# Row products of a scan step handed out one filler unit later, in a hybrid Mamba-2 / pooling trunk on one core

## The chip, the core and the metric

The kernel runs on one core of a Trainium2 chip. Five engines work side by side, each through its own queue in order: TensorE (PE in the profile, with its weight loads as PEld), VectorE (DVE), ScalarE (ACT), GpSimd (POOL) and SyncE (SP), which here issues most DMA transfers. The metric is the device time of one execution in microseconds (us); shown is the median of several runs. Beside these, one execution was profiled.

## The reference

The program is one step of a two-layer decoder trunk over 1024 prompt tokens and 64 sample tokens (8 sequences of 8), width 1024, all in float32. Layer 0 is a Mamba-2 (SSD) mixer, layer 1 a multi-scale causal pooling mixer; each is modulated by a conditioning vector, normalised, gated and added to the residual, and a final RMSNorm closes. What matters here is the chunked scan of layer 0, with 8 groups of 4 heads (head size 64, state size 128) and chunks of 128 tokens:

```python
acum = jnp.cumsum(dt * A, axis=2)
decay = jnp.where(mask, jnp.exp(seg), 0.0)          # seg = acum_t - acum_s
CB = jnp.einsum('bctgn,bcsgn->bctsg', C, B)
y_intra = jnp.einsum('bctsgr,bcsgrp->bctgrp', CB[..., None] * decay, xdt)
chunk_states = jnp.einsum('bctgn,bctgr,bctgrp->bcgrpn', B, decay_end, xdt)
def step(h, inp):
    s, d = inp
    return d[..., None, None] * h + s, h
y_inter = jnp.einsum('bctgn,bctgr,bcgrpn->bctgrp', C, jnp.exp(acum), h_prev)
y = y_intra + y_inter
```

Then come the skip term, a gate with silu(z), a group RMSNorm over 256 channels, and the output projection. The sample sequences run the same scan from a stored state.

## The kernel before

Activations lie with channels on the partitions and 1088 tokens (1024 + 64) along the free axis. Large products take float32 as a high and a low part, so one product is three matmuls (`mm1`, L190 to L192). The front of the kernel projects most columns; then the SSD stage (`ssd_layer`, L1547) runs the scan of the 8 groups, one after the other, while it deals out **filler units** between the scan's steps: pieces of big products that do not depend on the present scan. `beside` (L1589) yields them: first the input projections of the groups in BESIDE (one unit is one token chunk, 8 x 3 matmuls of 368 or 352 columns), the last tile of these in eight smaller units, and then the output projections by parts (one unit is 4 x 3 matmuls).

`scan_group` (L525) is a generator; each `yield` ends a **hand-out**, after which `ssd_layer` takes as many filler units as `FILL[g]` (L53) says at that place. Its pieces:
- `front(c)`, for a chunk of 128 tokens (c = 8 is the sample): the product of C and B (L573), transposes of x and B (L576) on PE; on ACT the decays as a Relu and an Exp (L581, L582), exp(acum) (L565) and a copy of the transposed B (Bt, L593); on DVE the masked C·B (L584), M (L587), the scaled x (xd, L589) and C times exp(acum) (ea, L602). M, xd and ea have three buffers, Bt two, the PSUM tile `tr` two. It also issues the load of acum two chunks ahead (L549, L552).
- `states(c)`, for the chunks c and c + 1: two products of Bt and xd into one PSUM tile S (L615), the decay of h on POOL (hd, L623), and the sum on DVE (L624, or a copy at L620 for a group's first).
- `rows(c)`, the **row products** of the same two chunks: M times xd (L637) and, into the same PSUM tile, h times ea (L641), with each half of 64 output rows in one half of the array; then DVE adds the skip term (L607). The first chunk uses the h from before `states(c)`, the second the first h made there.
- `sample_inter` (L645), `back_sample` (L663) and `state_sample` (L687) do the sample's part: the stored states times C (Z, L656), the sample's row products (L670) and its new states (L692, added at L695).
- After that the gate (L732), squares and their sum (zsum, L769), the mean square by PE (L741), the inverse root, and the scaled rows (L753), stored to DRAM (L756). The last two hand-outs of a group are taken as `rest` within the next group, after its first filler unit (L1564) and at its fourth hand-out (L1567).

The order of the instructions in each engine's queue is planned when the program is built, from the order of the program, the dependences and an estimate of when operands are ready; `issue_after` adds an edge to it by hand. So the order on an engine may differ from that of the program. The tiles of activations are slots of one list, taken from its head and returned to its end (`Slots`, L66). At one place (L1568) the loads of the next group's B, C and x into slots are issued, for the groups whose tiles were made early (5 and 7).

Of the kernel before, what the change touches and what calls it, by code (L numbers as in the profile page):

```python
# [49 lines left out]
         ("z", 7))  # L50
BESIDE = (1, 2, 3, 4, 6)

FILL = (((1,) * 10 + (2,),) * 4 + ((1,) * 9 + (4, 5),) + ((3, 2, 2, 2, 2, 2, 2, 2, 2, 2, 3),) * 2 + ((2, 2, 2, 1, 1, 1, 1, 1, 2, 2, 1),))  # L53
WIDE = 1223


# [43 lines left out]
class Build:  # L100
# [424 lines left out]
    def scan_group(self, g, T):  # L525
        nc, tk, gp, pp = self.nc, self.tk, self.gs, self.pp
        B, C, xs, zs = T[0], T[1], T[2:4], []
        hsl, h0 = [], []

        def load_z():  # L530
            for q in range(2):
                zs.append(self.slots.get("z"))
                nc.sync.dma_start(zs[q], self.zsd[2 * g + q])

        def load_h0():
            for i in range(2):
                t = self.slots.get("h0")
                nc.sync.dma_start(t[:, :1024], self.io["h0T"][g][:, 1024 * i:1024 * i + 1024])
                hsl.append(t)
                h0.append(t[:, :1024].rearrange("p (b r q) -> p b r q", b=4, r=4))  # L540
# [64 lines left out]
        def evac_y(py, q, tok, L):  # L605
            y = xs[q]
            nc.vector.scalar_tensor_tensor(out=y[:, tok], in0=y[:, tok], scalar=self.vec[:, V_D + 2 * g + q:V_D + 2 * g + q + 1], in1=py[:, :L],  # L607
                                           op0=ALU.mult, op1=ALU.add)

        def states(c, F):  # L610

            S = pp.tile([P, 512], F32, tag="S", bufs=1, name=self.name("S"))
            for i in range(2):
                xde, Bt = F[i][3:5]
                nc.tensor.matmul(S[:, 256 * i:256 * i + 256], Bt, xde.rearrange("p r q -> p (r q)"), start=True, stop=True)  # L615
            for i in range(2):
                cd, Si = F[i][5], S[:, 256 * i:256 * i + 256]
                hn = gp.tile([P, 4, 64], F32, tag="h", bufs=3, name=self.name("h"))
                if h[-1] is None:
                    ins = nc.vector.tensor_copy(hn.rearrange("p r q -> p (r q)"), Si)  # L620
                else:
                    hd = gp.tile([P, 4, 64], F32, tag="hd", bufs=1, name=self.name("hd"))
                    nc.gpsimd.tensor_tensor(out=hd, in0=h[-1], in1=cd.unsqueeze(2).to_broadcast([P, 4, 64]), op=ALU.mult)  # L623
                    ins = nc.vector.tensor_tensor(out=hn, in0=hd, in1=Si.rearrange("p (r q) -> p r q", r=4), op=ALU.add)  # L624
                h.append(hn)
            self.hins = ins.ins

        def rows(c, F):

            py = [pp.tile([P, 512], F32, tag="y", bufs=2, name=self.name("y")) for _ in range(2)]  # L630
            for i in range(2):
                tok, M, xdt, _, _, _, ct = F[i]
                hc, a = h[-3 + i], 128 * i
                for q in range(2):
                    for rr in range(2):
                        r, o = 2 * q + rr, slice(64 * rr, 64 * rr + 64)
                        nc.tensor.matmul(py[q][o, a:a + 128], xdt[:, r, :], M[:, r, :], start=True, stop=(hc is None))  # L637
                    if hc is not None:
                        for rr in range(2):
                            r, o = 2 * q + rr, slice(64 * rr, 64 * rr + 64)  # L640
                            nc.tensor.matmul(py[q][o, a:a + 128], hc[:, r, :], ct[:, r, :], start=False, stop=True)  # L641
            for q in range(2):
                evac_y(py[q], q, slice(128 * c, 128 * c + 256), 256)

        def sample_inter():  # L645

            ctm = self.ctm
            cv = C[:, NP:TOK].rearrange("p (j b i) -> p j b i", j=4, b=2)
            mv = ctm.rearrange("p (j b) k -> p j b k", b=2)
            nc.gpsimd.tensor_copy(mv[:, :, 0, 0:8], cv[:, :, 0, :])  # L650
            nc.gpsimd.tensor_copy(mv[:, :, 1, 8:16], cv[:, :, 1, :])
            Z = pp.tile([P, 512], F32, tag="S", bufs=1, name=self.name("Z"))
            for bb in range(2):
                for j in range(4):
                    b = 2 * j + bb
                    nc.tensor.matmul(Z[32 * j:32 * j + 32, :256], ctm[:, b, :], hsl[b // 4][:, 256 * (b % 4):256 * (b % 4) + 256],  # L656
                                     start=(bb == 0), stop=(bb == 1), tile_position=(0, 32 * j))
            zsc = gp.tile([P, 4, 64], F32, tag="hd", bufs=1, name=self.name("zsc"))
            nc.vector.tensor_tensor(out=zsc, in0=Z[:, :256].rearrange("p (r q) -> p r q", r=4),
                                    in1=self.eap[:, 4 * g:4 * g + 4].unsqueeze(2).to_broadcast([P, 4, 64]), op=ALU.mult)  # L660
            return zsc
# [44 lines left out]
        for c in range(0, 8, 2):  # L706
            states(c, F)
            if c == 6:
                load_z()
            Fn = [front(c + 2)]  # L710
            if c == 6:
                self.slots.free(B)
            rows(c, F)
            F = Fn
            if c == 6:
                zsc = sample_inter()
                self.slots.free(C)
            yield
            if c < 6:
                F.append(front(c + 3))  # L720
                if c == 4:
                    load_h0()
                yield
        F, h = F[0], h[-1]
        nc.sync.dma_start(self.io["hpT"][g], h.rearrange("p r q -> p (r q)"))
        st = back_sample(F, zsc)
# [820 lines left out]
    def ssd_layer(self):  # L1547
        nc, sl = self.nc, self.slots
        T, rest = {0: self.G[0]["out"]}, iter(())
        self.x = [None] * 8  # L1550
        self.acts = [[] for _ in PARTS]
        self.zadd = None
        self.prep = self.op_part_load(0, self.acts[0])
        self.fill = self.beside(T)
        for g in range(8):
            sc = self.scan_group(g, T[g])
            for i, n in enumerate(FILL[g]):
                next(sc)
                for j in range(n):
                    ins = next(self.fill)  # L1560
                    if ins:
                        self.zsum(ins)
                    if i == 0 and j == 0:
                        next(rest, None)  # L1564
                    elif i == 3 and j == 0:
                        with self.tc.issue_after(self.hins), self.tc.issue_after(ins.ins) if ins else contextlib.nullcontext():
                            next(rest, None)  # L1567
                if i == 8 and g + 1 in self.G:  # L1568
                    T[g + 1] = [sl.get("xbc") for _ in range(4)]
                    for t, d in zip(T[g + 1], self.xbd[g + 1]):  # L1570
                        nc.sync.dma_start(t, d)
            rest = sc
        self.prep = self.op_part_load(3, self.acts[3])
        self.out_unit()
        next(rest)
        for _ in range(2):
            next(self.fill)
        self.out_unit()
        for _ in rest:
            pass  # L1580
# [331 lines left out]
```

## Time and profile before

| | |
|---|---|
| Median of 3 runs | 1602.47 us (1600.35 to 1604.5) |
| Profiled execution, span from first to last instruction | 1599.4 us |
| Granted TensorE clock, mean | 0.999 |
| PE / DVE / ACT / POOL busy | 99% / 81% / 49% / 32% of the span |
| Scan stage (first to last of the scan's products) | about 345 to 915 us |

The profiled execution has no other time than its span; the timed runs contain what lies around it too. A line of the timeline gives the start, the duration, the engine, the line of the kernel and the operation, the tile written and those read, and how many instructions in a row were merged. A row of the groups gives the busy time, the mean duration and the idle time of the engine just before, with what ended it. Matmuls overlap in these records and their ends are modelled, so the distance between two starts says more than a duration.

### The profile page before, as it was taken

To read this page: it belongs to the slowest core of one execution; us is meant where nothing else is said; L and a number is where in the kernel's file an instruction comes from. 1 tells how busy PE (TensorE), PEld (TensorE's weight loads), DVE (VectorE), ACT (ScalarE), POOL (GpSimd) and SP (SyncE) were. 2 spreads that over 40 slices of the span, in tenths; PEclk is the share of its full clock that TensorE was granted. 3 is DMA by queue.
4 is the path that set the end of the run, shared out by engine and by line. 5 is a ranking of instruction groups with operands and counts; after the bars stand their busy time and mean duration, and the time that the engine had idled before them with its cause. 6 is when DMAs were issued, how large, how long until landed. Compare 5 with 4: busy or idle time off the path is not lost. (4 is left out here: it accounts for less than half of the span.)

```text
span 1599.4 us, 30692 instructions
## 1 busy us (share of the span) xinstructions
PE 1578.8 (99%) x11946; PEld 1505.4 (94%) x11946; DVE 1293.5 (81%) x2152; ACT 791.4 (49%) x1512; POOL 514.6 (32%) x558
## 2 busy tenths in 40 slices
PE   9999999999999999999999999999999999999997
PEld 7899999998889889888899899999999999999997
DVE  6874879778788888888989867998889867667886
ACT  6663344456676766675455437533323333233364
POOL 0133556512231313131212232275666640000241
PEclk9999999999999999999999999999999999999999
DMA  9423232355555554768899632142333279565683
GB/s 353 166 100 110 69 112 83 110 178 158 188 170 173 161 187 148 240 224 303 289 317 312 221 135 74 60 142 103 114 114 104 102 246 373 142 176 178 165 171 119
DMA packets 122305, 275.58 MB, mean 172 GB/s; under 512 B 18192, under 2 KB 59312, under 8 KB 122160
## 3 DMA queue, kind: packets, MB, share of 16 engines
q1 hardware_dynamic: 118128, 260.90, 47.3%
q0 software_dynamic: 4032, 12.72, 4.7%
q8 instruction: 94, 1.54, 0.4%
q14 instruction: 51, 0.42, 0.1%
HBM read 201.12 MB, written 70.23 MB: 170 GB/s over the span
## 5 line engine op out<-in xcount | busy, mean ns | idle before, releaser
L1051 PE MATMUL st<-hh,w 128*128 128x272 f32 x832 | 240.2, 289 | 0.9 <-ACT w L182 0.9
L1053 PE MATMUL st<-hh,w 128*128 128x272 f32 x832 | 240.4, 289 | 0.4 <-DVE w L184 0.4
L1052 PE MATMUL st<-hl,w 128*128 128x272 f32 x832 | 240.0, 288 | 0.0
L1051 PE MATMUL st<-t,w 128*128 128x272 f32 x624 | 179.7, 288 | 0.0
L1053 PE MATMUL st<-t,w 128*128 128x272 f32 x624 | 179.5, 288 | 0.0
L1052 PE MATMUL st<-t,w 128*128 128x272 f32 x624 | 179.2, 287 | 0.0
L190 PE MATMUL mm<-hh,wh 128*128 128x368 f32 (+1 forms) x528 | 178.3, 338 | 0.0
L192 PE MATMUL mm<-hh,wl 128*128 128x368 f32 (+1 forms) x528 | 173.7, 329 | 0.0
L191 PE MATMUL mm<-hl,wh 128*128 128x368 f32 (+1 forms) x528 | 173.1, 328 | 0.0
L1051 PEld LDWEIGHTS st<-hh,w 128*128 128x128 f32 x832 | 156.8, 188 | 1.4 <-ACT w L182 1.4
L1053 PEld LDWEIGHTS st<-hh,w 128*128 128x128 f32 x832 | 156.5, 188 | 0.9 <-DVE w L184 0.9
L1052 PEld LDWEIGHTS st<-hl,w 128*128 128x128 f32 x832 | 156.7, 188 | 0.0
L182 ACT ACTIVATE w<-wr 128x512 fp32r<-128x512 f32 x104 | 65.1, 631 | 166.2 <-PE st L1053 137.3
L623 POOL TENSOR_TENSOR hd<-h,cd 128x256 f32<-128x256 f32 x56 | 45.9, 820 | 301.0 <-DVE h L624 144.9
L1270 PE MATMUL op<-b,w 128*128 128x272 f32 x448 | 128.9, 288 | 0.8 <-DVE b L1199 0.7
L1269 PE MATMUL op<-b,w 128*128 128x272 f32 x448 | 129.5, 289 | 0.0
L1271 PE MATMUL op<-b,w 128*128 128x272 f32 x448 | 128.9, 288 | 0.0
L190 PE MATMUL mm<-gh,wh 128*128 128x368 f32 (+1 forms) x372 | 125.5, 338 | 0.0
L192 PE MATMUL mm<-gh,wl 128*128 128x368 f32 (+1 forms) x372 | 122.4, 329 | 0.0
L191 PE MATMUL mm<-gl,wh 128*128 128x368 f32 (+1 forms) x372 | 122.0, 328 | 0.2 <-DVE gl L783 0.2
L1051 PEld LDWEIGHTS st<-t,w 128*128 128x128 f32 x624 | 117.7, 189 | 0.1
L1053 PEld LDWEIGHTS st<-t,w 128*128 128x128 f32 x624 | 117.3, 188 | 0.0
(307 smaller groups left out, 4576.5 us busy)
## 6 DMA issues: line engine op xcount, KB each, us to landing
wr<-win SPq DMA_DIRECT2D x48, 512.0 KB, 4.2
acb<-acd SPq DMA_DIRECT2D x64, 256.0 KB, 4.4
wr<-pin SPq DMA_DIRECT2D x32, 512.0 KB, 3.5
wr<-pout SPq DMA_DIRECT2D x28, 512.0 KB, 4.3
x<-x1d SPq DMA_DIRECT2D x24, 544.0 KB, 5.9
x1d<-x SPq DMA_DIRECT2D x22, 544.0 KB, 3.9
wr<-pout POOLq DMA_DIRECT2D x20, 512.0 KB, 6.2
x<-xT SPq DMA_DIRECT2D x16, 544.0 KB, 6.3
```

What stands on the lines that cost most here:

```text
L182: self.nc.scalar.activation(hi, src, AF.Copy)
L190: nc.tensor.matmul(ps[:, :n], hi[:, k, :], ah[:, a:a + n], start=first, stop=False)
L191: nc.tensor.matmul(ps[:, :n], hi[:, k, :], al[:, a:a + n], start=False, stop=False)
L192: nc.tensor.matmul(ps[:, :n], lo[:, k, :], ah[:, a:a + n], start=False, stop=last)
L623: nc.gpsimd.tensor_tensor(out=hd, in0=h[-1], in1=cd.unsqueeze(2).to_broadcast([P, 4, 64]), op=ALU.mult)
L1051: nc.tensor.matmul(ps[c][:, :QUART], hi[:, k], xh[:, t], start=(k == 0), stop=False)
L1052: nc.tensor.matmul(ps[c][:, :QUART], hi[:, k], xl[:, t], start=False, stop=False)
L1053: nc.tensor.matmul(ps[c][:, :QUART], lo[:, k], xh[:, t], start=False, stop=(k == 3))
L1269: nc.tensor.matmul(ps[:, :QUART], hi[:, k], xh, start=k == 0, stop=False)
L1270: nc.tensor.matmul(ps[:, :QUART], hi[:, k], xl, start=False, stop=False)
L1271: nc.tensor.matmul(ps[:, :QUART], lo[:, k], xh, start=False, stop=k == 7)
```

## The change

In `scan_group`, the `yield` that followed `rows(c)` now precedes it: `states(c)` and `front(c+2)` form one hand-out, `rows(c)` and `front(c+3)` the next. For c = 6, where there is no `front(9)`, `rows(6)` and `sample_inter` form a hand-out of their own. A group has so 14 hand-outs, of which 12 lie within the group (11 before) and two are taken in the next. `FILL` deals the filler units anew over twelve places; the sums are the same for each group (12 in the first four, 18, 24, 24, 16). The loads for the next group are issued one place later.

```diff
-FILL = (((1,) * 10 + (2,),) * 4 + ((1,) * 9 + (4, 5),) + ((3, 2, 2, 2, 2, 2, 2, 2, 2, 2, 3),) * 2 + ((2, 2, 2, 1, 1, 1, 1, 1, 2, 2, 1),))
+FILL = (((1,) * 12,) * 4 + ((1,) * 9 + (2, 3, 4),) + ((2,) * 12,) * 2 + ((2, 2, 1, 1, 1, 1, 1, 1, 1, 2, 2, 1),))
...
             Fn = [front(c + 2)]
             if c == 6:
                 self.slots.free(B)
+            yield
             rows(c, F)
             F = Fn
-            if c == 6:
-                zsc = sample_inter()
-                self.slots.free(C)
-            yield
             if c < 6:
                 F.append(front(c + 3))
                 if c == 4:
                     load_h0()
-                yield
+            else:
+                zsc = sample_inter()
+                self.slots.free(C)
+            yield
...
-                if i == 8 and g + 1 in self.G:
+                if i == 9 and g + 1 in self.G:
```

## The prediction

> **What bounds the kernel now.** I read the page's busy shares first. TensorE (PE) is the bound: it is busy for all but 20.6 us of the span, so only what PE itself spends, idle or badly, can come out of the time.
>
> ```profile
> span 1599.4 us, 30692 instructions
> ## 1 busy us (share of the span) xinstructions
> PE 1578.8 (99%) x11946; PEld 1505.4 (94%) x11946; DVE 1293.5 (81%) x2152; ACT 791.4 (49%) x1512; POOL 514.6 (32%) x558
> ```
>
> Busy is not the same as well used: a matmul's end is modelled, so I went on to the timeline of PE and took the distances between starts. The stretch that the change touches is the scan, from about 345 to 915 us: eight scan groups, whose small products are dealt between the big products (`mm`) of the filler units. I write S for the state products (L615), T for a front's transposes and its C·B product (L573, L576), y for the row products (L637 with M, L641 with h). First group 0:
>
> ```profile
> 362.03 0.32 PE L191 MATMUL mm<-hl,wh 128*128 128x352 f32 x1
> 362.29 0.66 PE L641 MATMUL y<-ea,h 128*64 128x128 f32 x8
> 362.87 0.43 PE L192 MATMUL mm<-hh,wl 128*128 128x352 f32 x1
> 363.15 0.32 PE L190 MATMUL mm<-hh,wh 128*128 128x352 f32 x1
> ...
> 365.36 0.32 PE L192 MATMUL mm<-hh,wl 128*128 128x352 f32 x1
> 365.52 0.38 PE L573 MATMUL tr<-xbc,xbc 128*128 128x128 f32 x2
> 365.74 0.49 PE L576 MATMUL tr<-kc,xbc 128*128 128x128 f32 x3
> 365.99 0.41 PE L190 MATMUL mm<-hh,wh 128*128 128x368 f32 x1
> 366.24 0.33 PE L191 MATMUL mm<-hl,wh 128*128 128x368 f32 x1
> ...
> 369.75 0.33 PE L191 MATMUL mm<-hl,wh 128*128 128x368 f32 x1
> 369.92 0.33 PE L192 MATMUL mm<-hh,wl 128*128 128x368 f32 x1
> 370.08 1.02 PE L615 MATMUL S<-xd,Bt 128*128 128x256 f32 x4
> 370.95 0.38 PE L573 MATMUL tr<-xbc,xbc 128*128 128x128 f32 x2
> 371.17 0.49 PE L576 MATMUL tr<-kc,xbc 128*128 128x128 f32 x3
> 371.59 0.44 PE L637 MATMUL y<-M,xd 128*64 128x128 f32 x4
> ...
> 373.49 0.44 PE L190 MATMUL mm<-hh,wh 128*128 128x368 f32 x1
> 373.76 0.33 PE L191 MATMUL mm<-hl,wh 128*128 128x368 f32 x1
> ```
>
> The steady distances: an `mm` of 368 columns 0.17 us (369.75 to 369.92), one of 352 columns 0.16 by its width; four S 0.87 (370.08 to 370.95); a T 0.11 (two from 370.95 to 371.17); four y 0.22 (898.21 to 898.43, below). What an insertion costs beyond these is what it loses:
> - Five T alone, from the last `mm` before (365.36) to the second after (366.24): 0.88, less 0.16 + 0.17 + 0.55, is 0.00. T among `mm` is free.
> - A whole step S, T, y (32 y), 369.92 to 373.76: 3.84, less 0.34 + 0.87 + 0.55 + 1.76, is 0.32.
> - Eight y alone, 362.03 to 363.15: 1.12, less 0.32 + 0.44, is 0.36.
>
> So what loses time is each separate run of y, nearly whatever its length: 0.32 to 0.36 us. In many steps the row product of one step is cut into several:
>
> ```profile
> 433.70 0.32 PE L190 MATMUL mm<-hh,wh 128*128 128x352 f32 x1
> ...
> 435.63 0.70 PE L615 MATMUL S<-xd,Bt 128*128 128x256 f32 x2
> 436.26 0.87 PE L637 MATMUL y<-M,xd 128*64 128x128 f32 x10
> 437.06 0.43 PE L191 MATMUL mm<-hl,wh 128*128 128x352 f32 x1
> 437.42 0.66 PE L641 MATMUL y<-ea,h 128*64 128x128 f32 x8
> ...
> 655.28 0.70 PE L615 MATMUL S<-xd,Bt 128*128 128x256 f32 x2
> ```
>
> This is the first step of group 1: six y, the second S pair (which was not ready before), ten y, one `mm`, then the last eight y, which need h. From 433.70 to 437.42 are 3.72 us; less two `mm` 0.32, four S 0.87, five T 0.55 and sixteen y 0.88, it loses 1.10, where two runs at 0.32 and 0.36 would lose 0.68. The other 0.42 is stall. The same stands four times (groups 1 to 4; the last row is group 4's). The last row product and the places where PE openly waits for one:
>
> ```profile
> 358.72 0.66 PE L637 MATMUL y<-M,xd 128*64 128x128 f32 x8 [1.26 <-DVE M L587]
> ...
> 829.50 0.44 PE L641 MATMUL y<-ea,h 128*64 128x128 f32 x4 [1.01 <-DVE h L624]
> ...
> 898.21 0.39 PE L637 MATMUL y<-M,xd 128*64 128x128 f32 x4
> 898.43 0.39 PE L641 MATMUL y<-ea,h 128*64 128x128 f32 x4
> ```
>
> Between the first of these rows and the last I count 53 separate runs of y for 32 row products: 6, 7, 7, 7, 7, 9, 4, 6 in the eight groups.
>
> **The change part by part.** No instruction is added or removed, and each group gets as many filler units as before (12, 18, 24 or 16); only places move.
>
> *Row products one hand-out later.* Before, states(c), front(c+2) and rows(c) come together, so the y of M(c) and of the h just made follow S at once; h has then to pass POOL and DVE in the time of five T. After, a filler unit stands between: 24 `mm`, 24 x 0.17 = 4.1 us. Both open waits (1.26 and 1.01 us) are shorter than that, so 2.3 us go. A second S pair that is not ready leaves `mm` to run instead of y, and S among `mm`, like T, sits between full-array products; the four stalls of 0.42 go: 1.7 us. If every row product becomes one run, 53 - 32 = 21 runs fewer at 0.34 (the middle of 0.32 and 0.36): 7.1 us. Gross 11.1 us. What the y meets behind it is now T instead of `mm`; I price that junction at nothing, since an unbroken run is left the same way; its bounds are 0.1 either way for 24 steps, by the 0.10 that the first `mm` after y takes too long (373.49 to 373.76 is 0.27).
>
> Where the Trainium skill bears on this: its page TensorEngine Tiling (Array Packing), Key Properties, says that a change of tiling mode drains TensorE, and y (128x64) among full-array products is such a change. It speaks against a gain wherever a row product is whole already, and the rows agree (0.32 stays). But TensorE: Matmul & The Clock Gate, Step-by-step, puts the drain at about 128 cycles, 53 ns at its 2.4 GHz; two drains a run make 21 x 0.11 = 2.2 us (an estimate from that page) in place of 7.1, and the time would be about 1599.5. The trace's 0.36 for a lone run is the measurement, and I use it.
>
> *What is kept of the splits.* Group 5 has nine runs, in the stretch where the units turn from 4 us to 2 us and DVE and the loads are fullest. I leave its five surplus runs standing: 5 x 0.34 = 1.7 us back.
>
> *The tail of each group.* back_sample and state_sample come one hand-out later, and the mean-square product (L741) stands where it stood. It needs the DVE sum at L769:
>
> ```profile
> 790.64 1.28 DVE L769 TENSOR_TENSOR z<-z,z 128x1088 f32<-128x1088 f32 x1
> ```
> ```profile
> 793.01 0.67 PE L741 MATMUL ms<-z,ones 128*32 128x272 f32 x8
> ```
>
> In group 5 the sum ends at 791.92 and PE comes at 793.01: 1.1 us of cover. One op unit less lies between (3 become 2 at the end of the fill): 12 x 0.17 = 2.0 us. So the product would be 0.9 us late, unless other `mm` go ahead of it. Groups 5 and 6: 0 to 1.8, I take 1.0. In groups 0 to 4 the cover shrinks too, by a unit; I take nothing and keep 0.9 each, 4.5, for the range. Behind L741 on PE are only more `mm` and T, so a wait there is paid once.
>
> *front(c+3) now stands behind rows(c) in one hand-out.* M has three buffers, so ACT's four Relu of M(c+3) wait until y has read M(c):
>
> ```profile
> L581 ACT ACTIVATE M<-acb,tka 128x128 f32<-128x128 f32 x256 | 84.8, 394 | 18.9 <-PE y L637 15.0 <-DMA acb<-acd 3.1
> ```
>
> ACT already waits 15.0 us on that. Behind it in ACT's queue are the Bt copy (L593), which the next second S pair needs, and the evictions of `mm` (L434). From T to the next S there are 4.1 us of filler, as before; the Relus start when half the row product is done and take four times at most 0.39, so Bt is usually in time. Not at all, or 24 stalls of up to 1.26 (PE's longest wait on this chain): I take 0.5 us in all, near the lower end, because ACT is busy for 49% only.
>
> *The moved DMA issues.* The four loads of the next group's x/B/C (groups 4 and 6, from index 8 to 9) keep their place behind the freeing of C, so SP's queue holds for the same reason as before; they are one unit nearer to their use, with three or four hand-outs still between. load_h0 comes earlier relative to its product, the z loads too. Taken at nothing; a load that missed its group would cost what is left of its landing, once or twice.
>
> *Sum.* -2.3 -1.7 -7.1 +1.7 +1.0 +0.5 = -7.9 us. The profiled execution has a span of 1599.4, and 1591.5 after. The timed median is 1602.47, 3.1 us above that span (what lies around it); taking this as unchanged, 1594.6 us.
>
> **The rivals.**
> *Only the open waits go.* The planner splits row products at the new place as well, because M(c) and front(c+3)'s work now press on ACT and DVE together. For it: 81% DVE. Against: the splits stand where S or h was late, and these get 4.1 us. Time: 1602.5 - 2.3 = 1600.2.
> *It does not do what it says.* PE's order is planned by readiness, and the planner puts y where it put it before. Against: whole units stand between T and the next S in the rows above, in the order of the hand-outs. Time: 1602.5.
> *Slower: ACT stalls the second S pair.* One mechanism: in-order ACT waits at L581 for y, Bt comes late, PE stops at L615. It decides once the mean stall over the 24 steps passes 7.9 / 24 = 0.33 us; at half of the 1.26, 0.6 us, it costs 24 x 0.6 = 14.4, and the kernel comes to 1594.6 + 14.4 - 0.5 = 1608.5.
>
> **How the numbers follow.** The forecast has a chance of 0.62, its own range 1587 (no leftover runs, no losses, and the junction's 2.4: 1602.5 - 11.1 - 2.4 = 1589, and 2 us for the spread of the runs shown) to 1599 (the 4.5 of the other tails come on top). Only the waits 0.22, nothing 0.06, slower 0.10. About 0.3%, 4.8 us, is what a measurement of this kernel can tell from no change. Faster by more: nearly all of the forecast, 0.58, and 0.05 of the second case's edge, 0.63. Within: 0.03 + 0.16 + 0.05 = 0.24. Slower: 0.13, the slower rival and edges of the last two. The range for 8 in 10 runs from 1586.5 to 1603: it leaves out the slower rival and less than 0.1 below.
>
> **What would show it.** Right: about 32 to 40 runs of y, most of them between `mm` and T; no open wait before L637 or L641; the distance from one L741 to the next about 1.4 us shorter in groups 1 to 3 (three runs and one stall of 0.42 fewer); L573 and L615 still at no cost. Wrong: 50 or more runs of y; PE waiting at L615 for Bt or at L741 for z by more than 3 us together; ACT's wait on y at L581 far above 15 us with PE idle beside it; or a gain or loss outside 345 to 915 us.

## The result, and the profile after

The changed kernel takes 1604.26 us (median of 20 runs, 1601.33 to 1607.65) where the kernel before, run beside it on the same chip, takes 1601.57 us (20 runs, 1599.62 to 1604.86). The ratio is 1.0013, 95% interval 1.0007 to 1.0019: slower by 2 to 3 us. The forecast was 7.9 us faster. The profiled execution went from a span of 1599.4 to 1603.7 us.

The page of the changed kernel, busy shares:

```profile
span 1603.7 us, 30701 instructions
...
PE 1575.0 (98%) x11946; PEld 1507.6 (94%) x11946; DVE 1298.4 (81%) x2152; ACT 790.6 (49%) x1512; POOL 509.6 (32%) x558
```

PE is now idle for 28.7 us of the span, not 20.6. Read by stretches (busy us of PE, PEld, DVE, ACT and POOL; then the granted clock, the DMA share and GB/s), before in the first fence and after in the second, it is the scan that lost it:

```profile
345.00:915.00 570.00, 564.93 (x4346) 509.63 (x4345) 485.04 (x812) 353.07 (x806) 134.31 (x199) 1.00 0.67 224
```
```profile
345.00:915.00 570.00, 556.83 (x4320) 508.10 (x4319) 487.30 (x804) 351.19 (x804) 131.12 (x198) 1.00 0.67 222
```

The DMA is the same, and so is the mean clock to two digits; PE's idle time in the scan went from 5.1 to 13.2 us. DVE is busy for 85% of this stretch, which the 81% of the whole span hides.

The mean clock hides something too. Just after PE's longest wait in the scan (1.82 us, until 708.74, at the sample's row products of group 4) the granted clock falls to 0.50 for 3.41 us:

```profile
709.94:713.35 3.41, 3.41 (x13) 3.41 (x12) 3.41 (x4) 1.36 (x4) 3.41 (x2) 0.50 0.82 247
```

The `mm` start 0.29 to 0.31 us apart there, where 0.16 and 0.17 are usual, and about 1.5 us are lost. The profiled execution of the kernel before has no such stretch in its scan. Over the 20 runs of the changed kernel the mean clock is 0.9977, and 0.9980 over the 88 runs of the kernel before that stand beside the experiments below; 0.0003 of 1600 us is about 0.5 us, so the clock is a small part of the difference here.

What was to be mended is mended. This is the timeline of PE in the first step of group 1, the counterpart of the rows of before from 433.70:

```profile
435.64 0.32 PE L190 MATMUL mm<-hh,wh 128*128 128x352 f32 x1
435.81 0.70 PE L615 MATMUL S<-xd,Bt 128*128 128x256 f32 x2
...
437.41 0.70 PE L615 MATMUL S<-xd,Bt 128*128 128x256 f32 x2
437.75 0.51 PE L191 MATMUL mm<-hl,wh 128*128 128x352 f32 x1
438.11 0.32 PE L192 MATMUL mm<-hh,wl 128*128 128x352 f32 x1
438.35 0.88 PE L637 MATMUL y<-M,xd 128*64 128x128 f32 x12
439.06 0.39 PE L641 MATMUL y<-ea,h 128*64 128x128 f32 x4
439.28 0.39 PE L637 MATMUL y<-M,xd 128*64 128x128 f32 x4
439.49 0.39 PE L641 MATMUL y<-ea,h 128*64 128x128 f32 x4
439.81 0.49 PE L573 MATMUL tr<-xbc,xbc 128*128 128x128 f32 x2
440.14 0.49 PE L576 MATMUL tr<-kc,xbc 128*128 128x128 f32 x3
440.38 0.41 PE L190 MATMUL mm<-hh,wh 128*128 128x368 f32 x1
440.63 0.33 PE L191 MATMUL mm<-hl,wh 128*128 128x368 f32 x1
```

All 24 y are one run. From 438.11 to 440.63 are 2.52 us; less 0.16 and 0.17 for two `mm`, 1.32 for 24 y and 0.55 for five T, the run loses 0.32, the price that the prediction found for a run of y. The pair of S that was not ready now has `mm` beside it: 435.64 to 438.11 is 2.47, less five `mm` 0.80, four S 0.87 and five T 0.55: 0.25 lost, where the stall was 0.42. Over the whole scan there are 32 runs of y instead of 53, one for each row product, group 5 included.

And new waits stand elsewhere. PE's open waits in the scan (engine, line, waited for: us in total, times, longest), first before, then after:

```profile
PE mm L807 <- ACT raw L434: 1.7, 1, 1.7
PE y L637 <- DVE M L587: 1.3, 1, 1.3
PE y L641 <- DVE h L624: 1.0, 1, 1.0
PE S L615 <- ACT Bt L593: 0.5, 1, 0.5
PE Z L656 <- PE y L641: 0.3, 1, 0.3
```
```profile
PE y L670 <- POOL zsc L665: 4.3, 4, 1.8
PE tr L573 <- DVE h L695: 4.2, 4, 1.0
PE S L615 <- ACT Bt L593: 3.3, 5, 1.3
PE ms L741 <- DVE z L769: 1.2, 2, 0.8
```

For a balance I took, as in the prediction, the distance between starts at each insertion and subtracted the steady distances, and put what is left over, beyond the price of the runs, to the product at which the gap lies. In us, over the eight groups:

| | before | after | difference |
|---|---|---|---|
| separate runs of y (53, 32), at 0.34 | 18.0 | 10.9 | -7.1 |
| stalls within and before y | 4.1 | -1.1 | -5.2 |
| stalls at S | 2.0 | 5.6 | +3.7 |
| stalls at T, nearly all at a group's front(0) | 0.0 | 6.1 | +6.1 |
| stalls at the sample's row products (L670) | -0.5 | 4.5 | +5.0 |
| stalls at the mean square (L741) | 0.2 | 1.4 | +1.2 |
| everything else | 19.0 | 19.1 | +0.1 |
| lost in all | 42.8 | 46.6 | +3.8 |

(A negative stall is a run that cost a little less than the price assumed. At y before, 1.0 us is taken off that the sum counts twice where a single `mm` stands between two runs. Everything else is the price of the other small products among `mm`, and `mm` itself. It holds the wait for an eviction before, 1.7 us at L807, and the half clock after, about 1.5 us; that these nearly cancel is chance.) The scan is 3.8 us longer, 567.2 to 571.0, which is nearly the whole 4.3 us between the two spans; what lies behind the scan takes 685.2 and 685.5 us. So 12.3 us were won at the row products and 16.0 lost at four other places. By group the losses are 6.4, 5.1, 5.1, 5.1, 8.0, 5.8, 3.9, 3.4 before and 8.0, 5.9, 6.9, 5.9, 9.2, 4.1, 3.4, 3.2 after: groups 0 to 4 lose, 5 to 7 win. Group 4 has the L807 wait before and the half clock after.

How the two largest new stalls come about is seen at the end of group 2. In the changed kernel, PE, DVE and POOL:

```profile
557.71 0.33 PE L192 MATMUL mm<-hh,wl 128*128 128x368 f32 x1
559.70 0.45 PE L670 MATMUL y<-M,zsc 128*64 128x64 f32 x8 [1.66 <-POOL zsc L665]
...
571.72 0.49 PE L573 MATMUL tr<-xbc,xbc 128*128 128x128 f32 x2 [1.04 <-DVE h L695]
```
```profile
556.07 1.37 DVE L368 SCALAR_TENSOR_TENSOR raw<-raw,cwh,raw 128x1112 f32<-128x1112 f32 x1
557.36 0.42 DVE L659 TENSOR_TENSOR zsc<-Z,eap 128x256 f32<-128x256 f32 x1
...
560.12 3.05 DVE L368 SCALAR_TENSOR_TENSOR raw<-raw,cwh,raw 128x1112 f32<-128x1112 f32 x1
...
563.48 2.64 DVE L732 TENSOR_TENSOR xbc<-xbc,z 128x1088 f32<-128x1088 f32 x1
...
570.99 2.48 DVE L695 TENSOR_TENSOR h<-h,S 128x512 f32<-128x512 f32 x4
```
```profile
557.92 1.73 POOL L665 TENSOR_TENSOR zsc<-zsc,xd 128x256 f32<-128x256 f32 x1 [1.88 <-DVE zsc L659]
559.61 5.37 POOL L674 TENSOR_TENSOR h<-h,es 128x1024 f32<-128x1024 f32 x2
```

And the kernel before at the same place, DVE and POOL:

```profile
548.44 0.42 DVE L659 TENSOR_TENSOR zsc<-Z,eap 128x256 f32<-128x256 f32 x1
...
550.94 1.58 DVE L602 TENSOR_TENSOR ea<-xbc,ea 128x512 f32<-128x512 f32 x1 [1.48 <-ACT ea L565]
...
561.61 0.68 DVE L695 TENSOR_TENSOR h<-h,S 128x512 f32<-128x512 f32 x1
```
```profile
549.01 1.06 POOL L665 TENSOR_TENSOR zsc<-zsc,xd 128x256 f32<-128x256 f32 x1 [0.41 <-DVE zsc L659]
550.03 4.28 POOL L674 TENSOR_TENSOR h<-h,es 128x1024 f32<-128x1024 f32 x2
```

The sample's scaling zsc (L659) now falls behind the filler unit that closes a projected tile, and so behind that tile's convolution on DVE (L368). POOL's sum (L665) follows late and slowly (1.73 us, not 1.06), and PE waits 1.66 us. POOL's two decays of the stored sample states (L674) then run beside the convolutions instead of beside L602, and a convolution takes 3.05 us, not 1.37, and a gate (L732) 2.64, not 1.28. The sample's state sums on DVE (L695), which read the PSUM buffer that front(0) of the next group needs, came one by one from 561.61 on before; now they come at 570.99, and PE stops for 1.04 us more.

### The profile page after: what moved, and what is told of

Its sections match the earlier page's. It is cut to its first block, busy times and chain, and to the rows that moved or that the text cites. A ratio compares the mean times of both kernels' runs of the same rounds, so it can differ in the third digit from the quotient of the medians.

```text
span 1603.7 us, 30701 instructions
## 1 busy us (share of the span) xinstructions
PE 1575.0 (98%) x11946; PEld 1507.6 (94%) x11946; DVE 1298.4 (81%) x2152; ACT 790.6 (49%) x1512; POOL 509.6 (32%) x558
```

## The experiments

**Which of the moves does the harm.** Two kernels divide the change. The first hands the row products of c = 0, 2 and 4 out later and leaves c = 6, the tail of the group, FILL and the loads as before:

```diff
(against the kernel before)
             if c == 6:
                 self.slots.free(B)
+            else:
+                yield
             rows(c, F)
             F = Fn
-            if c == 6:
-                zsc = sample_inter()
-                self.slots.free(C)
-            yield
             if c < 6:
...
-                yield
+            else:
+                zsc = sample_inter()
+                self.slots.free(C)
+            yield
```

> rows(c) one hand-out later for c = 0, 2, 4 only; rows(6) and the sample's product stay with states(6), so the group's tail and the dealing of units are those of the kernel before. Theory A (joining the runs of y gains, the shifted tail gives it back): 32 runs of y, no wait of PE on zsc at L670 nor on DVE L695 at L573, and 5 to 8 us faster than before, about 1595. Theory B (the delay itself is worth nothing, waits only move to S and Bt): within 2 us of before.

The second moves only c = 6, with the FILL and the loads of the changed kernel:

```diff
(against the kernel before)
             if c == 6:
                 self.slots.free(B)
+                yield
             rows(c, F)
```

> The complement: rows(c) stays with states(c) for c = 0, 2, 4, and only rows(6) and the sample's product come one hand-out later, with the changed kernel's dealing of units. Theory A: all of the tail's loss and none of the gain, 53 or so runs of y, the waits at L670 and L573 of the changed kernel, 6 to 10 us slower than before, about 1610. Theory B: about the changed kernel's time, 1604.

Measured: 1601.66 against 1602.21 us, ratio 0.9993 (0.9984 to 1.0002), and 1606.81, ratio 1.0022 (1.0014 to 1.0031). The move at c = 6, with the new dealing and the later loads, costs 3.5 us: 52 runs of y, so nothing won, and 3.9 us of stalls at T. At the sample's row products PE has no wait in this kernel's list, although Z is as late as in the changed one: that stall needs the other three moves as well. The other three moves win runs (38 left) but no time: stalls at S are 7.1 us, at the sample's row products 2.9, at the products behind them (the sample's states and the mean square) 3.3. The time of the first is that of its Theory B, the time of the second lies between its two theories. So the tail is one cause and not the only one. In the first kernel DVE stood still at this place:

```profile
476.33 0.29 DVE L597 TENSOR_TENSOR Bl<-tr,Bt 128x128 fp32r<-128x128 f32 x1 [3.66 <-ACT Bt L596]
...
478.05 0.42 DVE L659 TENSOR_TENSOR zsc<-Z,eap 128x256 f32<-128x256 f32 x1
```

The copy of B (Bt) is late on ACT, and in DVE's queue the sample's zsc stands behind what needs it.

**The copy of B ahead of the Relus on ACT.** Three kernels with the same edit: on the changed kernel, on the first experiment, and, as a control, on the kernel before.

```diff
+            if c < 8:
+                Bt = gp.tile([P, 128], F32, tag="Bt", bufs=2, name=self.name("Bt"))
+                nc.scalar.activation(Bt, pt[:, 256:384], AF.Copy)
+            else:
...
             for r in range(4):
...
-            if c < 8:
-                Bt = gp.tile([P, 128], F32, tag="Bt", bufs=2, name=self.name("Bt"))
-                nc.scalar.activation(Bt, pt[:, 256:384], AF.Copy)
-            else:
...
```

> The changed kernel with the copy of the transposed B (Bt, L593) issued on ACT ahead of the Relus and the Exp of its front. Theory A (3.3 us of the loss are the second S pair waiting for Bt behind ACT's other work): the five waits at L615 go or halve, 2 to 4 us faster than the changed kernel. Theory B (Bt waits for the transposes or for xd on DVE, not for ACT's queue): no change at L615, within 1 us.

> Row products later for c = 0, 2, 4 only (tail and dealing as before) and the copy of the transposed B on ACT ahead of its front's Relus. Theory A' (what ate the gain of the joined runs of y is a tail brought nearer and Bt late behind ACT's queue; both are mended here): PE's stalls at S fall from 7 to about 3 us, those at the sample's products nearly go, 4 to 8 us faster than before, 1594 to 1598. Theory B' (DVE and ACT are the real bound of the scan, so a stall that is taken from PE at one place comes back at another): within 2 us of before, with as much stall in all as in the changed kernel.

> The control for it: the kernel before, with only the copy of the transposed B moved ahead of the Relus. Theory A': PE waits for Bt only 0.5 us in the kernel before, so within 1.5 us of it either way. Theory B': the same; this run only says how much of e6_c6_back_bt belongs to the copy alone.

Measured: 1603.02 against 1602.21 us, ratio 1.0002 (0.9994 to 1.0011); 1598.17 against 1600.83, ratio 0.9983 (0.9972 to 0.9993); and the control 1609.35 against 1600.83, ratio 1.0048 (1.0036 to 1.0060). The edit alone costs the old order about 8 us: PE waits at S for xd, 2.3 us, where it waited 0.5 for Bt, and at y 1.8 for h instead of 1.0; most of the loss is in groups 0 (6.4 to 8.5 us) and 7 (3.4 to 7.6). In this profiled execution each of these two groups also has 3.41 us at a clock of 0.5; but its mean clock over the five runs is that of the kernel before (0.998), so the clock does not make the 8 us. The expectation, 1.5 us at most, failed; why the edit costs so much is open. With the row products a unit later the same edit wins some 1.7 us, in both pairs (ratios 1.0013 to 1.0002 and 0.9993 to 0.9983); the intervals of each pair overlap, so this is likely and not certain. On the changed kernel that lies between the two theories. The stalls at S and at the sample's row products of the changed kernel shrink (5.6 to 3.6 and 4.5 to 1.5), those at T stay (5.5), since they have another cause. With the tail as before they are gone as well (0.5), and that kernel is the first that beats the kernel before, by 2.7 us where 4 to 8 were expected. But its stalls at S did not fall to the 3 us that its expectation named: PE waits there 4.3 us for xd, where it waited 4.6 us for Bt in the first experiment.

**The stall at the transposes: buffer or lateness.** The fourth PSUM tile of the sample's states, which front(0) waits for, is taken from the `mm` buffers:

```diff
-... for t, b in (("S", 1), ("y", 2), ("y", 2), ("tr", 2))]
+... for t, b in (("S", 1), ("y", 2), ("y", 2), ("mm", 3))]
```

> The changed kernel with the fourth state tile of state_sample taken from the three mm buffers of PSUM in place of the two tr buffers, so that the next group's transposes need not wait until DVE has added it (L695). Theory A (that wait is 4.2 us of the loss, 1.0 us in each of the groups 0 to 3): the wait at L573 goes, 3 to 5 us faster than the changed kernel. Theory B (DVE is late anyhow and PE then waits elsewhere, at mm or ms): less than 1.5 us.

Measured: 1605.6 against 1602.21, ratio 1.0020 (1.0011 to 1.0028). The wait for L695 at T is gone, but 2.6 us stay, now for DVE's convolved tile (L370), 6.9 us are lost between `mm` (3.8 before the edit) and 6.7 at the sample's row products. The 3.1 us more between `mm` fit the clock: behind three waits of about 2 us at L670 it is 0.5 for 3.41 us each, where the changed kernel has one such stretch, so that two more cost some 1.5 us each. So freeing the buffer gained nothing, as Theory B has it; that the buffer only passes on that DVE is late fits this.

**What makes DVE late.** POOL's decay of the stored sample states (L674) is left out, in the changed kernel and in the kernel before as a control; the sample's new states are then sums with undecayed ones, and all else is computed.

```diff
-            with self.tc.issue_after(ins.ins):
-                for i in range(2):
-                    nc.gpsimd.tensor_tensor(out=h0[i], in0=h0[i], in1=ea[...], op=ALU.mult)
```

> The changed kernel without GpSimd's two products per group that decay the stored sample states (L674), so the new sample states come out undecayed; everything else is computed. In the changed kernel these run beside the convolution on DVE, where single L368 take 3.05 us in place of 1.37. Theory C (GpSimd slows DVE there, and so the tail is late): the mean of L368 falls from 1.52 back to about 1.39 us, the wait of the next group's transposes for L695 falls by half or more, 3 to 5 us faster than the changed kernel. Rival (the place in DVE's queue alone makes the tail late): less than 1.5 us.

> The control: the kernel before without the same products of L674 (sample states undecayed). There they run beside the ea products (L602), which have slack. Theory C: within 1.5 us of before, so that the gain of e8_no_h0mul is due to the new place. Rival: any gain is the same here as in e8_no_h0mul.

Measured: 1599.95 and 1600.58 us against 1600.83, ratios 0.9993 (0.9983 to 1.0004) and 0.9996 (0.9987 to 1.0004). Against the kernel with the products, that is about 3 us for the changed order (from a ratio of 1.0013; the two intervals leave 1 to 5) and 0.6 us or nothing for the old one (its interval includes 1). The groups of convolutions on DVE, in the kernel before, the changed one, and the changed one without L674:

```profile
L368 DVE SCALAR_TENSOR_TENSOR raw<-raw,cwh,raw 128x1112 f32<-128x1112 f32 x60 | 83.3, 1388 | 1.9 <-ACT raw L366 1.6
```
```profile
L368 DVE SCALAR_TENSOR_TENSOR raw<-raw,cwh,raw 128x1112 f32<-128x1112 f32 x60 | 90.9, 1515 | 3.5 <-ACT raw L366 3.3
```
```profile
L368 DVE SCALAR_TENSOR_TENSOR raw<-raw,cwh,raw 128x1112 f32<-128x1112 f32 x60 | 82.5, 1375 | 5.8 <-ACT raw L366 5.5
```

The 7.6 us by which the changed kernel's convolutions are longer come from POOL's products beside them, and with these the stalls at T go from 6.1 to 0.6 us. (In the two kernels that divide the change, these convolutions take 82.5 us where the tail is as before and 91.5 where it alone is moved.) The stalls at the sample's row products do not go (5.9): that is a second mechanism. The Trainium skill, SBUF — State Buffer, SBUF: two separate sides, says that VectorE and GpSimd share one pair of ports, and that a VectorE operation with two inputs in SBUF and a GpSimd operation that reads SBUF exclude each other for a whole instruction. The rows agree in direction (both L368 and L674 are longer where they meet, 1.37 to 3.05 and 4.28 to 5.37 us); which of them held the ports is not seen in them.

**The sample's addition on DVE.** If POOL's start and pace at L665 were what PE waits for, the addition on DVE should help:

```diff
-            ins = nc.gpsimd.tensor_tensor(out=xz, in0=xz, in1=xdt, op=ALU.add)
+            ins = nc.vector.tensor_tensor(out=xz, in0=xz, in1=xdt, op=ALU.add)
```

> The changed kernel with the addition that readies the sample's row products (L665) on DVE instead of POOL. Theory: those row products wait (4.5 us in all) because the addition on POOL starts late and runs slowly beside DVE's convolutions; on DVE it follows the product before it at once, so 2 to 3 us of these stalls go, and POOL's decay of the sample states starts earlier, which takes up to 3 us more from the stalls of the transposes; 1599 to 1602. Rival: DVE itself is behind there, its queue only grows, and the stall stays or moves on to the mean square; 1604 to 1606.

Measured: 1621.35 against 1602.25 us, ratio 1.0118 (1.0103 to 1.0132). Both expectations fail, by far:

```profile
PE y L670 <- DVE zsc L665: 18.5, 6, 4.2
```
```profile
485.13 0.41 DVE L659 TENSOR_TENSOR zsc<-Z,eap 128x256 f32<-128x256 f32 x1
485.47 2.70 DVE L368 SCALAR_TENSOR_TENSOR raw<-raw,cwh,raw 128x1112 f32<-128x1112 f32 x1
488.09 0.42 DVE L665 TENSOR_TENSOR zsc<-zsc,xd 128x256 f32<-128x256 f32 x1
```

The addition does not follow the scaling at once: a convolution stands between them in DVE's queue, as one stands ahead of the scaling. It is the place in DVE's queue that is late, and an operation moved onto that queue gets one more such place. T has no stall in this kernel (0.6 us), but the sample's row products 20.3. And beside these waits, of up to 4.2 us, the clock falls to 0.5 in groups 1 to 4, for 20.5 us in all, of which PE is busy for 17.9. At 0.14 us lost of every 0.31 that is about 8 us (an estimate). Over its four runs the mean clock is 0.990, against 0.998 in the kernel before.

**The sample's product back at its old place.** In the changed kernel only `sample_inter` is handed out where it was before, ahead of the unit:

```diff
(against the changed kernel)
             if c == 6:
                 self.slots.free(B)
+                zsc = sample_inter()
+                self.slots.free(C)
             yield
...
-            else:
-                zsc = sample_inter()
-                self.slots.free(C)
             yield
```

> The changed kernel with only the sample's product Z and what it needs (L645 to L661) handed out where the kernel before did, ahead of the unit that now stands before the last row product; the row products, FILL and the rest as in the changed kernel. Theory: the stalls at the sample's row products (4.5 us) and at the transposes of the next group (6.1 us) come from Z falling behind the unit that closes a projected tile, so that its scaling on DVE stands behind a convolution and POOL's sums start late and run beside the convolutions; with Z early the former go to about nothing and the latter to 2 us at most, and the kernel comes to 1596 to 1598, 4 to 6 us faster than before. Rival: what counts is that the sample's row products and all behind them are one hand-out later whatever Z does; then the stalls at the transposes stay at 4 to 6 us and the time at 1602 to 1604.

Measured: 1604.36 against 1603.07 us, ratio 1.0009 (1.0000 to 1.0018). The stalls go as the theory has it, the time does not: it is not told apart from the changed kernel's 1.0013. Stalls at the sample's row products fall from 4.5 to 0.4 us and at T from 6.1 to 0.8, and groups 1 to 3 lose 4.3, 4.1 and 4.1 us, less than before the change (5.1 each). This kernel has the dealing and the loads of the changed one, so these do not make those stalls. But group 0 keeps its stalls at S (2.0 and 1.7 us), group 4 loses 8.3 us, about as before the change (8.0), and groups 6 and 7 lose 6.3 and 5.0 instead of 3.4 and 3.2. In group 6 PE waits for the sum of squares, and ahead of it ACT for a load (the line numbers of this part are one lower in this kernel: L740 is the mean square, L768 the sum):

```profile
PE ms L740 <- DVE z L768: 3.3, 1, 3.3
```
```profile
851.37 0.40 ACT L581 ACTIVATE M<-acb,tka 128x128 f32<-128x128 f32 x1 [12.73 <-DMA acb<-acd]
```

ACT's squares (L732 here) stand behind this Relu in its queue, so they, the split of the next weights and with it the sum on DVE (L768, at 859.13) come late; and behind PE's wait the clock is 0.5 for 3.41 us, part of group 6's loss. The load itself is not late: it is issued at 844.89, against 849.57 in the kernel before and 848.60 in the changed one. But in the kernel before ACT has its squares (852.12 and 853.88) ahead of the Relus of the next group (854.90). So here too it is a place in an in-order queue, ACT's this time. Why ACT's order came out so is open.

**Each group its own order.** Since the harm is done in groups 0 to 4 and the gain kept in 5 to 7, the last two kernels mix. The first has, in groups 0 to 4, the order with c = 6, tail and FILL as before, and in groups 5 to 7 the order and FILL of the changed kernel, with Bt first throughout. The second leaves group 0 wholly as before (its first entry of LATE_ROWS is all 0). The diff is the first one's, without FILL and Bt.

```diff
+LATE_ROWS = ((1, 1, 1, 0), (1, 1, 1, 0), (1, 1, 1, 0), (1, 1, 1, 0), (1, 1, 1, 0), (1, 1, 1, 1), (1, 1, 1, 1), (1, 1, 1, 1))
...
+            late = LATE_ROWS[g][c // 2]
+            if late:
+                yield
             rows(c, F)
...
-                if i == 8 and g + 1 in self.G:
+                if i == (9 if LATE_ROWS[g][3] else 8) and g + 1 in self.G:
```

> Groups 0 to 4 in the order of the kernel of before for c = 6, the tail and the filler, with the other row products later and Bt first (as in the sixth kernel); groups 5 to 7 with all row products later, the filler of the changed kernel and Bt first (as in the fourth kernel). Theory: what a group loses depends on that group's own order and on how full its units leave DVE and ACT, so the groups' losses add up: 7.8, 4.7, 3.8, 3.8 and 4.3 us measured for groups 0 to 4 there, 4.5, 2.6 and 2.5 us for groups 5 to 7 here, 33.9 in all against 42.8 before; 8 to 9 us faster, about 1593. Rival: the losses move from group to group (a stall avoided in one comes back in the next, because the chains of DVE and POOL run on), and the mix comes out like the better of its parts, 1598 to 1600.

> As the mix of groups, but group 0 wholly in the order of before, without Bt first (it lost 6.4 us before and 7.8 with the change). Theory: 1.4 us better than the mix, about 10 us faster than before, 1592. Rival: group 0's loss comes from the loads of acum, late whatever the order, or moves into group 1; then the same time as the mix within 1 us.

Measured: 1593.96 against 1602.25 us, ratio 0.9945 (0.9932 to 0.9957), and 1594.67, ratio 0.9958 (0.9945 to 0.9972). The mix is 8.3 us faster than the kernel before; its profiled span is 1590.4 us, and its scan has no stretch at half clock (mean clock over its runs 0.9986, against 0.9980: about 1 us of the 8.3). It loses 33.6 us in the scan where the sum over groups taken from two other kernels was 33.9; group by group it is less exact (5.8, 3.8, 3.8, 4.5, 4.4, 6.1, 2.4, 2.9). Group 0 in its old order gains nothing (7.1 us lost, not 6.4), so there the theory fell and the rival held.

## Why the prediction was wrong

Term by term:
- *Separate runs of y, -7.1, and five kept in group 5, +1.7.* The runs went from 53 to 32, group 5 included, and one joined run still costs 0.32: -7.1, nothing kept. The drain figure of the Trainium skill, TensorE: Matmul & The Clock Gate, Step-by-step, would have made it 2.2; the 0.32 measured for a run of the changed kernel stands against that. (The 1599.5 us that the prediction gave for this case kept the five runs of group 5 at 0.34; at 0.11 they cost 0.6, and it would be 1598.4.)
- *Open waits, -2.3, and hidden stalls inside y, -1.7.* All stalls at y went, 5.2 us. But a late second pair of S is not free among `mm`: 0.25 us of the 0.42 stayed in group 1, and in group 0 the wait did not go. (Some 0.1 of each 0.42 was no stall but the way into the next run of y: the lone run's first y starts 0.26 behind the `mm` ahead of it, not 0.16.) In group 0 PE waited 1.26 us for M and now waits 1.28 for Bt:

```profile
360.12 0.70 PE L615 MATMUL S<-xd,Bt 128*128 128x256 f32 x2 [1.28 <-ACT Bt L593]
```
```profile
355.44 1.28 ACT L581 ACTIVATE M<-acb,tka 128x128 f32<-128x128 f32 x4 [2.79 <-DMA acb<-acd]
```

  ACT had waited 2.79 us for acum (3.15 before the change); everything behind it is late, and it is only a matter of which product meets that first.
- *T behind y, 0 with bounds of 0.1.* Right: five T after a run of 24 y cost nothing beyond the 0.32.
- *Bt and the second pair of S, +0.5.* Measured +3.7 at S. This is the slower rival's place, but not its mechanism: ACT's wait for y at L581 fell, from 15.0 to 11.2 us, and five waits of 3.3 us in all, not 24, were enough.

```profile
L581 ACT ACTIVATE M<-acb,tka 128x128 f32<-128x128 f32 x256 | 86.4, 392 | 16.9 <-PE y L637 11.2 <-PE mm L192 2.9 <-DMA acb<-acd 2.8
```

- *The tail of each group, +1.0.* This is the step that failed. The prediction looked at the mean square alone, which took +1.2, about what was set down. It did not follow the two products of the tail that move with it: the sample's row products (+5.0) and, through the sample's states, the next group's first transposes (+6.1). What the moved steps issue was counted for DMA alone, and not for `sample_inter` and `back_sample`: their places in DVE's and POOL's queues, past the convolution of a closing tile, were not priced. The 4.5 us kept in the range for the other tails were for the same product, L741, and less than half of the 11.1. In place of 1.0 the tail cost 12.3 us.
- *Moved loads, 0.* No wait of PE for them is seen after the change.

So the gain was underestimated (12.3 us, where 9.4 was forecast), and the cost was 16.0 us where 1.5 was. Of the rivals, none named what happened. Of the signs named beforehand, 32 runs of y and no wait before L637 or L641 came as for right; L573 and L615 did not stay at no cost; and one sign of wrong came, PE's waits at L615 for Bt and at L741 for z, 4.5 us together.

What is shown: POOL's decays beside the convolutions make the stalls at T (gone without L674, and with Z early). The place of Z behind the closing unit has a part in those at the sample's row products (gone with Z early), but it makes none by itself: with only c = 6 moved, Z is as late and PE does not wait there. Bt behind the Relus is likely a part of the stalls at S: they went from 5.6 to 3.6 with Bt first on the changed kernel, but did not fall in the other pair. What stays open: the two stalls at S in group 0 (1.6 and 1.3 us), of which the late acum is seen and not tested; why the early Z changes ACT's order in group 6, and what hurts group 7; and why Bt first costs the old order so much. The new dealing of units was not run alone.

## What to carry to other kernels

Joining the pieces of a small product that changes the array's tiling was worth 0.3 us a piece here, and that part could be counted in advance. A step handed out later takes with it the places of all its operations in the in-order queues of DVE, POOL and ACT; where one of these is as busy as DVE here (85%), look in its timeline for the large operation that the small one will now stand behind, and for what will run beside it. Deal the order out group by group: the same move gained in groups 5 to 7 and lost in 0 to 4, and the mix, with Bt first, beat both kernels by half a per cent.

## What else the runs showed

A DVE operation of 1.37 us took 3.05 beside POOL's tensor products, and DVE's lateness then showed on PE some ten microseconds later, at a product of the next group. Behind some of PE's waits the granted clock was 0.5 for 3.41 us, which cost nearly as much as the wait: about 1.5 us after one of 1.82. Behind others it was not: the kernel before waits 1.7 us at L807, and the kernel with the moved PSUM tile 2.1 us at L615 in group 0. What decides it is not shown. Also unexpected: in eleven units of the changed kernel (some 210 products) the `mm` of 352 columns stood 0.167 us apart, as far as those of 368, instead of 0.158, at a granted clock of 1.00; before there is no such unit. This is 1.7 us of the scan, its cause is open. Two stretches of the changed kernel, six `mm` each:

```profile
418.39 0.32 PE L192 MATMUL mm<-hh,wl 128*128 128x352 f32 x1
...
419.34 0.32 PE L192 MATMUL mm<-hh,wl 128*128 128x352 f32 x1
```
```profile
567.60 0.33 PE L190 MATMUL mm<-hh,wh 128*128 128x352 f32 x1
...
568.60 0.33 PE L190 MATMUL mm<-hh,wh 128*128 128x352 f32 x1
```
